# Diagonal blocks masked a strip at a time in a 2-D prefix-sum kernel, and a rearranged end

## The chip, the cores and the metric

The kernel runs on one core of one Trainium2 chip. The metric is the device time of one execution in microseconds, the median of several. A profile's span is about 1.7 us shorter than the time of the same run. Of the engines, TensorE does the matrix products, into an accumulator memory called PSUM; VectorE and ScalarE multiply, add and sum along rows; GpSimd issues the loads. The input is fp32 in memory; the kernel's strips hold it as bf16, a format of two bytes.

## The reference, cut to what matters

```python
B, H, W = 4, 4224, 4224                       # x is fp32
ps = np.cumsum(np.cumsum(x, axis=1), axis=2)
diag = np.diagonal(ps, axis1=1, axis2=2)
return np.cumsum(diag, axis=1)
```

Each of the four images must be read once: 4 x 4224 x 4224 x 4 bytes = 285.5 MB. The output is 68 KB. The diagonal at i needs the sum of every element whose row and column are both at most i; an element (r, c) first counts at max(r, c). The output is the running sum of that diagonal.

## The kernel before

A strip is 768 rows: 128 partitions, six rows each. It is loaded as bf16 (the load casts) by GpSimd's queue into one of three buffers. For a strip that starts at row r0, columns right of its diagonal block go through TensorE into column sums; columns left of it are summed along rows by ScalarE and VectorE; and the block on the diagonal is split by a mask `um` into the part above the diagonal (into the column sums) and the rest (into the row sums).

```python
NBUF = 3
strips = ctx.enter_context(tc.tile_pool(name="strips", bufs=NBUF))
mup = ctx.enter_context(tc.tile_pool(name="mup", bufs=3))
...
def masked(o, i, m, acc):                      # product and its row sums in one instruction
    nc.vector.scalar_tensor_tensor(out=o, in0=i, scalar=1.0, in1=m,
                                   op0=ALU.mult, op1=ALU.mult, accum_out=acc)
...
def add_up(strip, f, r0, acc, ums, wp=0, ws=None):
    nw = f * P // GW
    g = r0 // GW
    hi = r0 + f * P
    for j in range(g + nw, NG):                # right of the block: TensorE
        for q in range(f):
            columns(j, 0, GW, strip[:, q, j * GW : (j + 1) * GW])
    ...
    for q in range(f):                         # the block, one of the f rows at a time
        mu = mup.tile([P, F2 * P], BF16, name="mu")[:, : f * P]
        masked(mu, strip[:, q, r0:hi], ums[q], acc[:, q, 2:3])
        for h in range(nw):
            columns(g + h, 0, GW, mu[:, h * GW : (h + 1) * GW])
        if ws > wp:
            act_sum(acc[:, q, 0:1], strip[:, q, wp:ws])          # ScalarE
    row_sums(acc[:, :, 1], strip[:, :, ws:hi])                   # VectorE, masked part included
```

Later the masked sums are taken off again (`acc[..., 1] - acc[..., 2]`). TensorE works in program order: the masked matmuls of a strip stand behind all its unmasked ones (in the first strip of the old profile the 54 unmasked start at 36.06 us, the first masked one at 47.71). The six products of a strip share three `mu` buffers, so the fourth waits for TensorE to have read the first.

The last 128 rows of the last image come at the very end, in four blocks of 32 rows (0 to 3). They add to the last 128 outputs, and the 256 rows ahead of them to the last 384, through small one-row matmuls (`weigh`) in three PSUM tiles `fin_a`, `fin_m` and `fin_e`.

## Time and profile before

| what | value |
|---|---|
| time, median of 3 | 668.58 us |
| span of the profile | 666.7 us |
| load queue's busy share | 99.8% |
| VectorE busy | 335.7 us (50%) |
| TensorE busy | 215.4 us (32%) |
| ScalarE busy | 140.2 us (21%) |
| a full load, from issue to landing | 69.2 us, median |

How to read it: the engines are idle half of the time or more, and the transfers never are. The GB/s in the slices that follow count the bytes that land, as bf16 (142.47 MB for the load queue); the bytes read, in fp32, are twice that (285.47 MB), so that 217 GB/s there are 434 GB/s of reads. A load that takes 69 us to land, while one lands every 30 us, has spent more than half of that standing behind other loads. The wait that the change aims at is in the wait view of the old kernel (who waited for whom: total us, times, longest us):

```profile
DVE mu L257 <- DMA strip<-in_x_dram: 217.6, 20, 21.3
DVE mu L257 <- PE d L214: 91.2, 16, 9.5
```

The first line is VectorE waiting for data. The second is VectorE stopped in the middle of a strip's products until TensorE has freed a `mu` buffer.

### The profile page before, as it was taken

The numbers are of one execution on the slowest core, as the hardware profiler recorded it, in microseconds if no ns is written. First come the engines' busy times: TensorE is split into PE (matmuls) and PEld (weight loads), VectorE is DVE, ScalarE is ACT, GpSimd is POOL, SyncE is SP. The second block draws the span as 40 slices with busy tenths as digits, with TensorE's granted clock in tenths as the row PEclk, the third lists the DMA queues.
The fourth block names the chain that finished last, engine by engine and source line by source line (L and its number), as shares of the span: only waits on it lengthen the run. The fifth ranks groups of instructions, "written<-read, shape, count | busy, mean of one in ns | idle before, by whom it ended". The sixth has DMA issues, their size and how long they took to land.

```text
span 666.7 us, 2921 instructions
## 1 busy us (share of the span) xinstructions
PE 215.4 (32%) x1009; PEld 99.4 (15%) x1009; DVE 335.7 (50%) x381; ACT 140.2 (21%) x226; POOL 28.0 (4%) x61
## 2 busy tenths in 40 slices
PE   0071623403118153140321724404032254350426
PEld 0030211101003021010110312201011021120103
DVE  3023627276924351745782425265498241635776
ACT  0000121406300103040630020304063002030436
POOL 5000000000000000000000000000000000001000
PEclk9995858566558585765655958667565595765759
DMA  9999999999999999999999999999999999999998
GB/s 201 219 219 219 214 219 218 211 217 213 218 220 219 216 217 219 216 217 219 214 216 216 216 219 217 220 211 219 217 217 219 213 220 215 217 217 217 215 210 154
DMA packets 7673, 143.27 MB, mean 215 GB/s; under 512 B 702, under 2 KB 1002, under 8 KB 2154
## 3 DMA queue, kind: packets, MB, share of 16 engines
q0 software_dynamic: 7296, 142.47, 99.8%
q1 hardware_dynamic: 362, 0.61, 0.3%
q8 instruction: 8, 0.13, 0.1%
q14 instruction: 7, 0.06, 0.0%
HBM read 285.47 MB, written 0.07 MB: 428 GB/s over the span
## 4 chain that ended last, share of the span: by engine, by line
another core or an unknown queue 39%; DVE 24%; PE 21%; DMA 12%; issue 4%; POOL 0%; DVEq 0%; POOLq 0%
PE d L214 21%; DVE acc L240 16%; DMA strip<-in_x_dram 12%; DVE mu L257 6%; POOL strip L420 0%; DVE pu L240 0%; DVE c L257 0%; POOL strip L409 0%; DVE acc L343 0%; DVE acc L340 0%; PE carry_ps L214 0%; DVE rows L368 0%; DVEq L257 0%; PE fin_e L214 0%
## 5 line engine op out<-in xcount | busy, mean ns | idle before, releaser
L257 DVE SCALAR_TENSOR_TENSOR mu<-strip,um 128x768 bf16<-128x768 bf16 (+1 forms) x129 | 110.7, 908 | 308.9 <-DMA strip<-in_x_dram 217.6
L214 PE MATMUL d<-strip,sel 128*11 128x384 bf16 x603 | 138.9, 404 | 333.8 <-DMA strip<-in_x_dram 333.8
L235 ACT ACTIVATE dump<-strip 128x416 bf16<-128x416 bf16 (+8 forms) x112 | 128.3, 1146 | 523.0 <-DMA strip<-in_x_dram 520.3
L240 DVE TENSOR_REDUCE acc<-strip 128x6 f32<-128x4608 bf16 (+6 forms) x23 | 195.9, 8519 | 0.0
L214 PEld LDWEIGHTS <-sel 128*11 128x11 bf16 x849 | 86.2, 102 | 512.9 <-issue 475.3
L214 PE MATMUL d<-mu,sel 128*11 128x384 bf16 x243 | 59.6, 354 | 65.7 <-DVE mu L257 65.5
L76 POOL DMA_DIRECT2D strip<-in_x_dram x24 | 16.4, 686 | 555.9 <-DVE acc L240 415.4
L235 ACT ACTIVATION_READ_ACCUMULATOR dump<-strip 128x1 f32 x112 | 20.9, 186 | 0.0
L214 PE MATMUL d<-ident,rows 128*11 128x128 f32 x24 | 5.2, 379 | 17.2 <-DVE rows L377 16.4
L257 DVE DVE_READ_ACCUMULATOR mu<-strip,um 128x1 f32 x129 | 10.6, 82 | 0.0
L214 PE MATMUL fold<-strip,ident_h 128*128 128x480 bf16 x8 | 3.3, 589 | 8.6 <-DMA strip<-in_x_dram 8.6
L214 PEld LDWEIGHTS d<-ident,rows 128*11 128x11 f32 x24 | 2.5, 119 | 19.1 <-DVE rows L377 17.3
L214 PE MATMUL d<-halves,rows 128*11 128x64 f32 x48 | 5.3, 290 | 0.0
L214 PEld LDWEIGHTS d<-halves,rows 128*11 128x11 f32 x48 | 4.7, 127 | 1.8 <-issue 1.7
L240 DVE TENSOR_REDUCE pu<-d 11x1 f32<-11x384 f32 x4 | 2.2, 545 | 5.0 <-PE d L214 5.0
L214 PE MATMUL fold<-weights,quarter 32*128 32x128 f32 x2 | 0.8, 498 | 11.0 <-POOL quarter L200 11.0
L447 DVE TENSOR_TENSOR_SCAN c<-ones_row,carry,c 11x384 f32<-11x384 f32 x4 | 4.0, 1006 | 0.1
L447 DVE TENSOR_TENSOR_SCAN c<-ones_row,carry,d 11x384 f32<-11x384 f32 x4 | 4.0, 1001 | 0.1
L214 PEld LDWEIGHTS <-ident_h 128*128 128x128 bf16 x20 | 2.2, 114 | 12.0 <-issue 11.9
L420 POOL DMA_DIRECT2D strip<-in_x_dram x5 | 2.7, 552 | 21.5 <-DMA strip<-in_x_dram 21.5
L240 DVE TENSOR_REDUCE parts<-strip 128x3 f32<-128x3072 bf16 x1 | 3.4, 3350 | 0.0
L221 DVE COPY weights<-fold 128x128 f32<-128x128 f32 x1 | 0.3, 291 | 5.4 <-PE fold L214 5.4
(102 smaller groups left out, 44.4 us busy)
## 6 DMA issues: line engine op xcount, KB each, us to landing
strip<-in_x_dram POOLq DMA_DIRECT2D x19, 6336.0 KB, 69.2
strip<-in_x_dram POOLq DMA_DIRECT2D x5, 3168.0 KB, 55.2
strip<-in_x_dram POOLq DMA_DIRECT2D x1, 1080.0 KB, 45.0
strip<-in_x_dram POOLq DMA_DIRECT2D x1, 768.0 KB, 48.0
strip<-in_x_dram POOLq DMA_DIRECT2D x3, 256.0 KB, 49.2
head<-in_x_dram SPq DMA_DIRECT2D x1, 528.0 KB, 3.9
strip<-in_x_dram POOLq DMA_DIRECT2D x1, 192.0 KB, 43.7
strip<-in_x_dram POOLq DMA_DIRECT2D x1, 64.0 KB, 28.6
```

The source lines that it names most:

```text
L76: nc.gpsimd.dma_start(out=o, in_=x[b, r0 : r0 + f * P, :].rearrange("(p f) w -> p f w", f=f))
L214: nc.tensor.matmul(o, lhsT=lhsT, rhs=rhs, start=start, stop=False, skip_group_check=True)
L221: nc.vector.tensor_copy(out=weights4, in_=w4_ps)
L235: nc.scalar.activation(out=dump[:, :w], in_=src, func=ACT.Copy, accum_out=acc)
L240: nc.vector.reduce_sum(out=acc, in_=src, axis=AX.X)
L257: nc.vector.scalar_tensor_tensor(out=o, in0=i, scalar=1.0, in1=m, op0=ALU.mult, op1=ALU.mult, accum_out=acc,)
L420: nc.gpsimd.dma_start(out=part_b[:, sb, c0:c1], in_=x[b, r0 : r0 + R, :TB].rearrange("r (k c) -> r k c", k=4)[:, :, c0:c1],)
L447: nc.vector.tensor_tensor_scan(out=c12[:, i, :], data0=ones_row, data1=src, initial=carry[:, i : i + 1], op0=ALU.mult, op1=ALU.add,)
```

## The change

The intent: fewer and longer VectorE instructions with no wait on TensorE in mid-strip; one PSUM row of 384 columns (`fin`) and one of 32 (`fin_e`) in place of three pieces at the end; block 1 of the last rows summed by ScalarE and VectorE instead of TensorE. The core of the diff:

```diff
-    mup = ctx.enter_context(tc.tile_pool(name="mup", bufs=3))
+    mup = ctx.enter_context(tc.tile_pool(name="mup", bufs=1))
...
-            for q in range(f):
-                mu = mup.tile([P, F2 * P], BF16, name="mu")[:, : f * P]
-                masked(mu, strip[:, q, r0:hi], ums[q], acc[:, q, 2:3])
+            mu = mup.tile([P, f, f * P], BF16, name=f"mu{f}")
+            block = strip[:, :, r0:hi]
+            nc.vector.tensor_mul(out=mu, in0=block, in1=um)
+            nc.vector.tensor_sub(out=block, in0=block, in1=mu)
+            for q in range(f):
                 for h in range(nw):
-                    columns(g + h, 0, GW, mu[:, h * GW : (h + 1) * GW])
+                    columns(g + h, 0, GW, mu[:, q, h * GW : (h + 1) * GW])
...
-            nc.vector.tensor_sub(
-                out=acc[..., 1], in0=acc[..., 1], in1=acc[..., 2]
-            )
...                                             (the end)
-        fin_a = psum_s.tile([1, M0], FP32, name="fin_a")
-        fin_m = psum_s.tile([1, E0 - M0], FP32, name="fin_m")
+        fin = psum_s.tile([1, GW], FP32, name="fin")
...
-        for sb, cp in ((0, CB), (1, c1a)):
-            for c in range(0, cp, P):
-                matmul(by_ps[:, sb * R :], part_b[:, sb, c : c + P], ...)
+        for c in range(0, CB, P):
+            matmul(by_ps, part_b[:, 0, c : c + P], weights4_h, start=c == 0)
...
+        for k, ca in ((0, 512), (1, 448)):      # blocks 1 and 2
+            act_sum(bsum[:, k, 0:1], part_b[:, k + 1, :ca])
+            pair_sum(bsum[:, k, 1:2], part_b[:, k + 1, ca:])
+            if k == 1:
+                finish(0, M0)
+            row_sums(btot[:, k : k + 1], bsum[:, k])
+            weigh(btot[:, k : k + 1], weights4, M0 + (k + 1) * R)
```

The difference is written back into the strip, so the plain row reduction that follows needs no correction. The mask tile now holds all six rows' masks (4608 columns instead of 773). Left out of the cut: each pair sum writes into a tile of its own instead of a shared one, and the sums of the 256 rows in `fold_a` take 256 columns of a row in one matmul instead of 128.

More of the change, by code (lines that the diff above doesn't have):

```diff
@@ L91, in upper_mask @@
     def upper_mask(f):
-        w = f * P
-        wide = consts.tile([P, w + f - 1], BF16, name=f"um{f}")
-        nc.vector.memset(wide, 1.0)
+        um = consts.tile([P, f, f * P], BF16, name=f"um{f}")
+        nc.vector.memset(um, 1.0)
         nc.gpsimd.affine_select(
-            out=wide,
-            in_=wide,
+            out=um,
+            in_=um,
             compare_op=ALU.is_gt,
             fill=0.0,
-            base=1 - f,
-            pattern=[[1, w + f - 1]],
+            base=0,
+            pattern=[[-1, f], [1, f * P]],
             channel_multiplier=-f,
         )
-        return [wide[:, f - 1 - q : f - 1 - q + w] for q in range(f)]
+        return um
     um6 = upper_mask(F2)
@@ L240, in row_sums @@
         nc.vector.reduce_sum(out=acc, in_=src, axis=AX.X)
+    pairs = []
     def pair_sum(acc, src):
         w = src.shape[-1] // 2
-        pair = dumpool.tile([P, 512], FP32, name="pair")
+        pair = last.tile([P, 288], FP32, name=f"pair{len(pairs)}")
+        pairs.append(pair)
         nc.vector.scalar_tensor_tensor(
@@ L312, in columns, with add_up @@
             first[0] = False
-        def add_up(strip, f, r0, acc, ums, wp=0, ws=None):
+        def add_up(strip, f, r0, acc, um, wp=0, ws=None):
             nw = f * P // GW
@@ L332, in add_up @@
             row_sums(acc[:, :, 1], strip[:, :, ws:hi])
-        acc6 = smalls.tile([P, NS, F2, 3], FP32, name="acc6")
-        acc3 = smalls.tile([P, 2, F, 3], FP32, name="acc3")
+        acc6 = smalls.tile([P, NS, F2, 2], FP32, name="acc6")
+        acc3 = smalls.tile([P, 2, F, 2], FP32, name="acc3")
         nc.vector.memset(acc6[:, 0, :, 0], 0.0)
@@ L388 @@
             fold_in(fold_g, strip[:, F:], 0, wp, 160, start=True)
-            parts = last.tile([P, F, 4], FP32, name="parts")
+            parts = last.tile([P, F, 3], FP32, name="parts")
             add_up(strip[:, F:], F, T0 - GW, parts, um3, wp, ws)
-            nc.vector.tensor_scalar_mul(
-                out=parts[:, :, 2], in0=parts[:, :, 2], scalar1=-1.0
-            )
-            row_sums(parts[:, :, 3], fold_g)
+            row_sums(parts[:, :, 2], fold_g)
             row_sums(r3[:, row_of(LG - 1), :], parts)
@@ L425 @@
                 )
-            fold_a = psum_s.tile([P, 2, P], FP32, name="fold_a")
+            fold_a = psum_s.tile([P, 2, 256], FP32, name="fold_a")
             c0, c1 = acuts[0]
             cp, ca = c0 + 768, c0 + 768 + 1152
-            fold_in(fold_a, part_a, c0, cp, P, start=True)
+            fold_in(fold_a, part_a, c0, cp, 256, start=True)
             for h in range(2):
@@ L465 @@
         cp = c0 + 768
-        fold_in(fold_a, part_a, c0, cp, P)
+        fold_in(fold_a, part_a, c0, cp, 256)
         for h in range(2):
@@ L475 @@
         E0 = GW - R
-        fin_a = psum_s.tile([1, M0], FP32, name="fin_a")
-        fin_m = psum_s.tile([1, E0 - M0], FP32, name="fin_m")
+        fin = psum_s.tile([1, GW], FP32, name="fin")
         fin_e = psum_s.tile([1, R], FP32, name="fin_e")
         yl = last.tile([1, GW], FP32, name="yl")
-        def weigh(rows, w, r0, fins, start=False):
-            for fin, f0, f1 in fins:
-                g0 = max(f0, r0)
-                if g0 < f1:
-                    matmul(
-                        fin[:, g0 - f0 :], rows, w[:, g0 - r0 : f1 - r0], start=start
-                    )
@@ L490, in finish, with weigh @@
-        def finish(fin, c0, c1):
+        def weigh(rows, w, r0, start=False):
+            matmul(fin[:, r0:], rows, w[:, : GW - r0], start=start)
+        def finish(c0, c1):
             nc.vector.tensor_add(
-                out=yl[:, c0:c1], in0=fin, in1=c12[0:1, 1, c0:c1]
+                out=yl[:, c0:c1], in0=fin[:, c0:c1], in1=c12[0:1, 1, c0:c1]
             )
         by_ps = psum_s.tile([P, P], FP32, name="fold")
-        c1a = CB // 2
-        for sb, cp in ((0, CB), (1, c1a)):
-            for c in range(0, cp, P):
-                matmul(
-                    by_ps[:, sb * R :],
-                    part_b[:, sb, c : c + P],
-                    weights4_h[:, : P - sb * R],
-                    start=sb == 0 and c == 0,
-                )
@@ L507 @@
-        bsum = last.tile([P, 3], FP32, name="bsum")
-        act_sum(bsum[:, 0:1], part_b[:, 1, c1a:])
+        for c in range(0, CB, P):
+            matmul(by_ps, part_b[:, 0, c : c + P], weights4_h, start=c == 0)
         by = last.tile([P, P], FP32, name="by")
         nc.scalar.copy(out=by, in_=by_ps)
-        fins = ((fin_a, 0, M0), (fin_m, M0, E0), (fin_e, E0, GW))
-        weigh(arows[:, 0:1], weights, 0, fins[:1], start=True)
-        weigh(arows[:, 1:2], weights, P, fins[:1])
-        weigh(arows[:, 0:1], weights, 0, fins[1:], start=True)
@@ L516 @@
-        weigh(arows[:, 1:2], weights, P, fins[1:])
-        weigh(dtot, weights, M0, fins)
-        weigh(bsum[:, 0:1], weights4, M0 + R, fins)
-        weigh(ones_col, by, M0, fins)
-        finish(fin_a, 0, M0)
-        act_sum(bsum[:, 1:2], part_b[:, 2, :448])
-        pair_sum(bsum[:, 2:3], part_b[:, 2, 448:])
-        for k in (1, 2):
-            weigh(bsum[:, k : k + 1], weights4, M0 + 2 * R, fins)
+        weigh(arows[:, 0:1], weights, 0, start=True)
+        weigh(arows[:, 1:2], weights, P)
@@ new lines @@
+        weigh(ones_col, by, M0)
+        weigh(dtot, weights, M0)
+        bsum = last.tile([P, 2, 2], FP32, name="bsum")
+        btot = last.tile([P, 2], FP32, name="btot")
+        for k, ca in ((0, 512), (1, 448)):
[5 more added lines that the diff above has]
+            weigh(btot[:, k : k + 1], weights4, M0 + (k + 1) * R)
@@ L533 @@
         for k in (1, 0, 2):
-            weigh(esum[:, k : k + 1], weights4, E0, fins)
-        finish(fin_m, M0, E0)
+            matmul(fin_e, esum[:, k : k + 1], weights4[:, :R], start=k == 1)
+        finish(M0, GW)
         nc.sync.dma_start(
@@ L538 @@
         )
-        finish(fin_e, E0, GW)
-        nc.sync.dma_start(out=out[b, T0 + E0 : N].unsqueeze(0), in_=yl[:, E0:])
+        ye = last.tile([1, R], FP32, name="ye")
+        nc.vector.tensor_add(out=ye, in0=fin_e, in1=yl[:, E0:])
+        nc.sync.dma_start(out=out[b, T0 + E0 : N].unsqueeze(0), in_=ye)
 _INS = ['x']
```

## The prediction

> **What bounds the kernel now.** I read the page's slices first, because they tell whether one resource is full all the time. The columns are 40 equal slices of the 666.7 us span; the digits are tenths of busy time, then GB/s.
>
> ```profile
> DVE  3023627276924351745782425265498241635776
> ...
> DMA  9999999999999999999999999999999999999998
> GB/s 201 219 219 219 214 219 218 211 217 213 218 220 219 216 217 219 216 217 219 214 216 216 216 219 217 220 211 219 217 217 219 213 220 215 217 217 217 215 210 154
> ...
> q0 software_dynamic: 7296, 142.47, 99.8%
> ```
>
> The transfers are full in every slice, VectorE is half idle. A strip of 768 rows by 4224 fp32 columns is 12.98 MB of reads. In the chain of work (start, duration, what) the first strips land where the piece before TensorE's matmuls ends:
>
> ```profile
> 1.33 34.69 DMA strip<-in_x_dram
> 36.06 12.15 PE d L214 x56
> ...
> 65.95 8.93 PE d L214 x44
> ...
> 95.94 7.34 PE d L214 x32
> ...
> 125.81 5.81 PE d L214 x20
> ```
>
> The landings are 29.9 us apart, which is 12.98 MB / 29.9 us = 434 GB/s. They do not come closer while the engines idle: between 15 and 35 us nothing computes, and the transfers run as they do later.
>
> The next question is whether a transfer ever waits for a buffer. The wait view blames VectorE for long idle times of GpSimd, which issues the loads, but an issue is late only if the queue has run dry. The timeline of GpSimd gives the issues:
>
> ```profile
> 56.36 0.77 POOL L76 DMA_DIRECT2D strip<-in_x_dram  x1 [45.42 <-DVE acc L240]
> ...
> 146.26 0.70 POOL L76 DMA_DIRECT2D strip<-in_x_dram  x1 [29.96 <-DVE acc L240]
> 175.06 0.71 POOL L76 DMA_DIRECT2D strip<-in_x_dram  x1 [28.10 <-DVE acc L343]
> ```
>
> At 56.36 the strips landing at 65.95 and 95.94 are already queued: 39.6 us of spare time. The tightest are 146.26, where the half strip behind the landing at 155.68 should end near 170.6 (half of 29.9 later), 24 us to spare, and 175.06, where the next strip lands at 200.57, 25 us. So no buffer ever limits the transfers. The end, from the same chain:
>
> ```profile
> 619.74 43.68 DMA strip<-in_x_dram
> ...
> 663.51 0.29 DVE pair L246
> ...
> 663.97 0.57 PE fin_e L214 x6
> ...
> 664.56 0.18 DVE yl L491
> ```
>
> The last data count as landed at 663.4, and the span ends 3.3 us later. Only three things can move the time: the transfers' start, their rate, and these 3.3 us.
>
> **What the Trainium skill says.** "VectorE: DVE Perf Modes", section "The perf-mode tier table", gives a bf16 tensor_tensor in SBUF two elements a cycle (1224 ns for 2048) and tensor_reduce one. The page's fp32 tensor_tensor formula, (N+151)/0.96 ns, fits this trace's one-element-a-cycle operations: 957 for 768 elements against 955 ns measured for the masking product, 4957 for 4608 against 4950 for the reduction. This trace has no large bf16 tensor_tensor, so its double rate is unconfirmed here. "DMA: Bandwidth & Descriptors", section "Where 436 GB/s comes from", puts the ceiling of the core's transfer ports at 435 GB/s; the trace has 434, so the stream is at it. "SBUF — State Buffer", section "SBUF: two separate sides", says that engine and DMA accesses use disjoint ports, and warns that GpSimd cannot write descriptors while VectorE holds a shared port in a two-port mode; a two-input VectorE operation holds it only against a GpSimd operation that reads SBUF. The even landings agree with the first. The old product has two SBUF inputs too, so the change adds no new kind of holding.
>
> **The change, part by part.** *Masks.* Removed are 114 products of 768 columns and 15 of 384 with their 129 accumulator reads: 103.1 + 7.6 + 10.6 = 121.3 us. Added are, for 19 strips and 5 three-row pieces, one product and one difference each. At two elements a cycle I estimate from the skill's figure (2304+151)/0.96 = 2.56 us and, for 1152 elements, 0.76 us: 38 x 2.56 + 10 x 0.76 = 104.9 us. The larger mask tiles cost (5760 - 1159)/0.96 ns = 4.8 us more of memset at the start. VectorE goes from 335.7 to about 319 us. What matters more, its wait in mid-strip goes: the old product cycles through three buffers and waits for TensorE (91.2 us in 16 waits in the wait view), the new one has a tile for the whole strip. In the first strip the reduction would end at 36.04 + 2 x 2.56 + 4.95 = 46.1 instead of 55.8. The buffer then waits for TensorE instead: its masked matmuls begin at 47.7, and twelve at 0.19 us (1.14 us for six) end at 50.0. The next load is issued some 6 us earlier, behind 46 us of queued transfers instead of 39.6. It lands when it did before. Gain: 0.
>
> *Setup.* The masks' select on GpSimd covers 5760 elements instead of 1159, which took 1.31 us: about 6.5, so 5.2 more, plus some 3 us of waiting for the longer memset. GpSimd's constants end near 19 instead of 11 us, long before the first landing at 36, and behind the three first loads. Cost: 0.
>
> *The end.* The landings of the last blocks stay near 661.2, 662.5, 663.45 and, for the last quarter-width piece, some 0.3 later. Block 1 now costs ScalarE 0.63 + 0.19 us and VectorE about 0.4 us beside each other, ready at 662.1 by the rows of the timeline, and a small reduction of 0.17 us. TensorE loses four matmuls of block 1 and the split of each weighing in up to three: the one-row sums are 384, 256, 128 and 128 columns. The old 256 + 128 columns began at 661.52 and were over at 662.06; in that proportion 896 columns need 1.26 us. They can begin at 661.0, when the row totals exist, because block 1's matmuls no longer stand ahead: done by 662.3. Then on VectorE: block 2's pair sum 662.6 to 663.05; the first 256 outputs, which now stand behind it (0.41 us, before it in the old order), to 663.45; a small reduction to 663.6, where ScalarE's sum is ready at 663.24; then the two pair sums of block 3, 0.1 later than before; the addition of 128 outputs beside TensorE's last matmul; and the last addition of 32. Sum for the tail: +0.1 us, within -0.1 and +0.6.
>
> Together 668.6 + 0 + 0.1 = **668.7 us**.
>
> **Rivals.** (1) *VectorE's saving comes out in the time.* For it: releases come earlier, and the chain gives VectorE 24%. It would mean up to 16 us, 652 us. Against it: 24 us to spare at the tightest issue, and the transfers already at 434 GB/s. I give it hardly a chance. (2) *The double rate does not come.* Each product or difference costs 4.96 us, VectorE rises to about 407 us (61%). Per strip that is 9.9 instead of 5.9 us, 4 us later at most, inside the 24 us. Only the last three-row piece, at 649.9, could push on: 1.3 us there, which reach the row totals at 661.9 instead of 660.9. The time would be 669 to 669.7. (3) *GpSimd is shut out while VectorE runs the long two-input operations.* A few us on an issue with 24 to spare: 0. (4) *VectorE's new order at the end exceeds the landings' spacing of 1.2 us.* The four last operations are back to back; each further wait on TensorE or ScalarE adds 0.2 to 0.4: 669.2.
>
> **Range and chances.** The runs before spread from 668.11 to 668.94. To this I add the tail, -0.1 to +1, and as much again as the runs' spread for the transfers of another session: 667.4 to 670.0. A change of over 2% is 13 us. Faster would need fewer bytes or a higher rate, slower a dry queue; the changed kernel moves the same bytes in the same order. 1% faster, 98% within, 1% slower.
>
> **What would show it right or wrong.** Right: 29.9 us between landings, 99.8% for the load queue, the first landing at 36.0; two VectorE rows of about 2.56 and 0.76 us; no wait of the product on TensorE in mid-strip; loads issued about 6 us earlier after the first strip with a longer median from issue to landing; last data near 663.4, end of span 3.2 to 3.9 us later. Wrong: landings further apart than 30.1 us, a slice of the transfers below 9 before the last, rows of 4.9 us, or a tail above 4 us, where the wait just ahead of the last additions names the term.

## The result

The changed kernel takes 668.48 us (median of 6 runs, 667.20 to 671.07), the old one beside it 668.55 (6 runs, 668.10 to 669.11). The ratio is 1.000, 95% interval 0.998 to 1.002. A ratio here and below is the mean time of one kernel's fast runs over that of the other's of the same rounds, so it is not quite the ratio of the medians quoted. Executions over 1.5% slower than the fastest of the same kernel are left out of the means. The change is worth nothing that these runs can see.

The slices of the changed kernel's page, span 665.7 us, answer to those of the old one in the prediction:

```profile
DVE  3161625456916153454782524436288333352867
...
DMA  9999999999999999999999999999999999999998
GB/s 203 219 219 219 219 218 218 219 209 212 219 221 218 218 218 219 218 218 216 209 218 220 218 216 218 219 218 218 218 213 215 219 217 215 219 217 218 218 205 161
...
q0 software_dynamic: 7296, 142.47, 99.9%
```

The transfers are as full as before and their bytes are the same. On VectorE, the instruction groups (count, then busy us and the mean ns of one, then idle time before them and what ended it):

```profile
L329 DVE TENSOR_TENSOR mu<-strip,um 128x4608 bf16<-128x4608 bf16 x19 | 48.6, 2558 | 300.7 <-DMA strip<-in_x_dram 300.7
L330 DVE TENSOR_TENSOR strip<-strip,mu 128x4608 bf16<-128x4608 bf16 x19 | 48.6, 2558 | 0.9
```

The predicted 2.56 us is 2558 ns. All the idle time ahead of the product is for data; the 91.2 us for TensorE are gone. The timeline of GpSimd (start, duration, the idle time ahead and what ended it) shows what this does to the loads:

```profile
46.66 0.78 POOL L76 DMA_DIRECT2D strip<-in_x_dram  x1 [29.49 <-PE d L213]
...
142.36 0.70 POOL L76 DMA_DIRECT2D strip<-in_x_dram  x1 [31.48 <-DVE acc L239]
174.33 0.72 POOL L76 DMA_DIRECT2D strip<-in_x_dram  x1 [31.27 <-ACT dump L234]
```

What gave the first of these buffers back shows in TensorE's timeline (first the unmasked matmuls, which read the strip, then the masked ones, which read the `mu` tile):

```profile
34.86 11.50 PE L213 MATMUL d<-strip,sel 128*11 128x384 bf16 x54 [16.85 <-DMA strip<-in_x_dram]
46.20 2.11 PE L213 MATMUL d<-mu,sel 128*11 128x384 bf16 x12
```

The first strip landed at 34.8 us, and its buffer was given back 11.8 us later; in the old kernel it was 56.36 - 36.06 = 20.3 us. The earlier issue bought nothing. The page's list of loads (count, KB, median us from issue to landing), first of the old kernel, then of the changed one:

```profile
strip<-in_x_dram POOLq DMA_DIRECT2D x19, 6336.0 KB, 69.2
```

```profile
strip<-in_x_dram POOLq DMA_DIRECT2D x19, 6336.0 KB, 76.5
```

By the median, the loads are issued some 7 us earlier and stand 7 us longer in the queue. They land every 29.9 us either way (single gaps are longer, in both: at most 30.15 us between two neighbouring full strips of the old profile, 30.54 of the changed one). That is where the gain went.

### The profile page after: what moved, and what is told of

The parts are those of the page before. It is cut to its first block, busy times and chain, and to the rows that moved or that the text cites. A ratio compares the mean times of both kernels' runs of the same rounds, so it can differ in the third digit from the quotient of the medians.

```text
span 665.7 us, 2561 instructions
## 1 busy us (share of the span) xinstructions
PE 204.8 (31%) x979; PEld 98.2 (15%) x979; DVE 334.6 (50%) x166; ACT 140.3 (21%) x226; POOL 32.0 (5%) x61
## 4 chain that ended last, share of the span: by engine, by line
DVE 47%; another core or an unknown queue 44%; DMA 5%; PE 2%; issue 1%; DVEq 0%; POOLq 0%
DVE acc L239 29%; DVE mu L329 8%; DVE strip L330 8%; DMA strip<-in_x_dram 5%; PE d L213 1%; DVE c L445 1%; PE fold L213 1%; DVE pu L239 0%; PE fin L213 0%; DVE c L259 0%; DVE rows L369 0%; DVE acc L344 0%; PE carry_ps L213 0%; DVE carry L443 0%
## 5 line engine op out<-in xcount | busy, mean ns | idle before, releaser
L329 DVE TENSOR_TENSOR mu<-strip,um 128x4608 bf16<-128x4608 bf16 (+1 forms) x24 | 52.4, 2183 | 305.8 <-DMA strip<-in_x_dram 305.7
L213 PE MATMUL d<-mu,sel 128*11 128x384 bf16 x243 | 49.1, 355 | 45.8 <-DVE mu L329 45.8
L330 DVE TENSOR_TENSOR strip<-strip,mu 128x4608 bf16<-128x4608 bf16 (+1 forms) x24 | 52.4, 2183 | 1.0
L213 PE MATMUL fold<-strip,ident_h 128*128 128x480 bf16 x8 | 3.4, 598 | 10.6 <-DMA strip<-in_x_dram 10.6
L213 PE MATMUL fold<-weights,quarter 32*128 32x128 f32 x2 | 0.8, 496 | 17.2 <-POOL quarter L199 17.2
L94 DVE MEMSET um<- 128x4608 bf16 (+1 forms) x2 | 4.9, 2458 | 1.1 <-issue 1.1
L95 POOL TENSOR_SCALAR_AFFINE_SELECT um<-um 128x4608 bf16<-128x4608 bf16 (+1 forms) x2 | 5.2, 2608 | 2.4 <-DVE um L94 2.4
## 6 DMA issues: line engine op xcount, KB each, us to landing
strip<-in_x_dram POOLq DMA_DIRECT2D x19, 6336.0 KB, 76.5
```

What stands on the lines that cost most here:

```text
L94: nc.vector.memset(um, 1.0)
L95: nc.gpsimd.affine_select(out=um, in_=um, compare_op=ALU.is_gt, fill=0.0, base=0, pattern=[[-1, f], [1, f * P]], channel_multiplier=-f,)
L213: nc.tensor.matmul(o, lhsT=lhsT, rhs=rhs, start=start, stop=False, skip_group_check=True)
L329: nc.vector.tensor_mul(out=mu, in0=block, in1=um)
L330: nc.vector.tensor_sub(out=block, in0=block, in1=mu)
```

## The experiments

Eleven experiments ran, the last of them the changed kernel once more, all correct, on three chips. "Old" is the kernel before, "changed" the kernel after.

### Each half of the change alone, and the wait alone

*e1_masks_only*: the new masks with the old end.

```diff
 (old, with)
+            nc.vector.tensor_mul(out=mu, in0=block, in1=um)
+            nc.vector.tensor_sub(out=block, in0=block, in1=mu)
 (and the rest of the masks; everything from fold_a on, and pair_sum, as in the old kernel)
```

> The new masks with the old end. Theory (the stream of transfers sets the time and has 24 us to spare at its tightest): 668.5 us within the runs' spread, landings 29.9 us apart, VectorE busy about 334 us, loads of full strips landing some 76 us after their issue as in the changed kernel (69 in the old). Rival (the masks gain and the new end gives it back): 665 or less here, and more than 670 with the new end alone.

*e2_tail_only*: the old masks with the new end.

```diff
 (old, with everything from fold_a on, and pair_sum, as in the changed kernel)
+        fin = psum_s.tile([1, GW], FP32, name="fin")
```

> The old masks with the new end. Theory: 668.5 us within the runs' spread, last landing to end of span 3.2 to 3.4 us as in both kernels, loads landing 69 us after issue. Rival (the new end costs what the masks gain): over 670. If the first landing at 34.8 us (36.0 in the old kernel) belongs to the longer setup of the new masks, it is near 36.0 here and near 34.8 with the new masks; if it is chance, it is in no order.

*e3_six_mu*: one line of the old kernel.

```diff
-    mup = ctx.enter_context(tc.tile_pool(name="mup", bufs=3))
+    mup = ctx.enter_context(tc.tile_pool(name="mup", bufs=6))
```

> The old kernel with six mask buffers instead of three, nothing else. Theory: VectorE's wait on TensorE in mid-strip (91.2 us in 16 waits) goes almost wholly, loads land about 76 us after their issue instead of 69, and the time stays 668.5. Rival (those 91 us are on the path): tens of us faster.

Measured, beside the old kernel's 668.87 us (11 runs, 668.15 to 671.08): masks alone 669.60 (ratio 1.0003, 0.9986 to 1.0020), end alone 668.20 (0.9989, 0.9976 to 1.0003), six buffers 669.65 (1.0007, 0.9989 to 1.0024). All three are the same as the old kernel. So no gain of one half is eaten by a loss of the other.

In e1 and in e3 VectorE's wait for TensorE in mid-strip is gone from the wait view, and in both a full load takes longer from issue to landing: 76.5 and 76.4 us, against 70.0 in e2, which keeps the old masks. The only wait of the product that is left in e3, and its list of loads:

```profile
DVE mu L257 <- DMA strip<-in_x_dram: 311.7, 20, 22.1
...
strip<-in_x_dram POOLq DMA_DIRECT2D x19, 6336.0 KB, 76.4
```

One line moves the loads as much as the whole new masking does, and neither moves the time. VectorE's busy time in e1 is 333.8 us, as expected.

### More bytes

*e4_more_bytes*: the changed kernel, one more load of 128 rows per whole image into rows that nothing reads.

```diff
             load_rows(strip[:, :F], b, T0)
+            load_rows(strip[:, F : F + 1], b, 0)
```

> The changed kernel with 2.163 MB more read per whole image, into rows of a strip buffer that nothing reads (three loads, 6.49 MB, no further work for an engine). Theory: 6.49 MB at 434 GB/s are 14.95 us, so 683.4 us. Rival (an engine or a wait for a buffer sets the time, the stream has slack): clearly less than 15 us more, down to 0.

Measured: 683.01 us (682.25 to 684.05), 14.1 us above the old kernel's 668.87 of the same call (ratio 1.0204, so 13.6 us by the means; interval 12.4 to 14.9). Nearly all of the 14.95 us that the bytes take at 434 GB/s appears in the time. The transfers are the bound; in a kernel bound by an engine the added bytes, on which no engine works, should have cost little.

### More work for VectorE

*e5_after_two*: the changed kernel, two useless reductions per full strip.

```diff
+            if f == F2:
+                waste = dumpool.tile([P, F2], FP32, name="waste")
+                for _ in range(2):
+                    row_sums(waste, strip[:, :, r0:hi])
             row_sums(acc[:, :, 1], strip[:, :, ws:hi])
```

> The changed kernel with two reductions of 4608 elements more per full strip, 4.95 us each: 19 x 9.9 = 188 us more of VectorE, 80% busy. Theory: 668.5 us still, since VectorE's work per image, about 85 + 50 = 135 us, stays below the 164.6 us that an image's transfers take. Rival (VectorE's work is on the path at least in part): anything from 10 to 188 us more.

Measured: 673.80 us (672.50 to 675.16) beside 669.23, ratio 1.0065 (1.0041 to 1.0089). Of 188 us more work, about 4.5 us come out in the time. The expectation, that none would, was wrong, and the timeline of VectorE in the changed kernel, without the extra work, says why:

```profile
643.67 0.17 DVE L386 COPY rows<-acc 128x3 f32<-128x3 f32 x1
648.85 0.76 DVE L329 TENSOR_TENSOR mu<-strip,um 128x1152 bf16<-128x1152 bf16 x1 [5.01 <-DMA strip<-in_x_dram]
```

Here VectorE has finished the last full strip and the first three-row piece and waits 5.01 us for the last piece. That is all its spare time at the end. The last full strip's 9.9 us more push 4.9 us past it. In e5's own profile TensorE shows the landing of that piece, and VectorE comes to it 4.75 us later:

```profile
650.70 3.36 PE L213 MATMUL fold<-strip,ident_h 128*128 128x480 bf16 x8 [0.85 <-DMA strip<-in_x_dram]
```

```profile
655.45 0.76 DVE L329 TENSOR_TENSOR mu<-strip,um 128x1152 bf16<-128x1152 bf16 x1
```

What comes after then runs late to the end of the span. The landings stay 29.9 us apart (650.70 is 1.9 us later than in the changed kernel's profile only because the first landing was, 36.79 for 34.86). An average over an image, which is what I had computed, hides this: a strip in mid-stream has the next strips to make up for it, the last one has not.

*e6_after_five* and *e7_before_five*: the same with five reductions, in the changed kernel and in the old one, so that VectorE is the bound.

```diff
-                for _ in range(2):
+                for _ in range(5):
```

> The changed kernel with five such reductions per full strip, 24.8 us: VectorE's work per image is about 208 us, above the 164.6 us of its transfers, so that VectorE must become the bound. Theory: about 830 us, VectorE over 95% busy, transfers no longer full. It is run to be compared with the old kernel under the same load.

> The old kernel with the same five reductions per full strip. With VectorE as the bound, the difference from the changed kernel is what the change saves of VectorE. Theory from the start-to-start times of the records (six products 0.885 us apart, 5.31 us, against a product and a difference of 2.60 each, 5.19): 19 x 0.12, the rest small, 2 to 4 us longer than the changed kernel under the same load. As in the prediction (accumulator reads counted as time of their own): 16 us longer. If the mid-strip wait on TensorE persists under this load: up to 91 us longer; I expect it gone, since TensorE has its unmasked columns done before VectorE comes to the strip.

Measured: 846.62 us for the changed kernel (846.06 to 847.37) and 882.57 for the old one (881.71 to 883.83). Under this load the change is worth 36 us. The expectation for the old kernel was an excess of 2 to 4. (The 830 us expected for the changed one took VectorE as busy throughout; it idled for 43 us of the span, from 801.5 to 844.8.) From the two pages, e6 first, then e7: line 1 (busy us and share of the span) and VectorE's slices.

```profile
PE 220.0 (26%) x979; PEld 102.3 (12%) x979; DVE 801.5 (95%) x261; ACT 140.2 (17%) x226; POOL 32.0 (4%) x61
...
DVE  4399999999989999999998999999999899999997
```

```profile
PE 239.6 (27%) x1009; PEld 101.0 (11%) x1009; DVE 801.7 (91%) x476; ACT 140.2 (16%) x226; POOL 28.0 (3%) x61
...
DVE  2189999999969999999995999999999699979997
```

VectorE does the same amount of work in both, 801.5 and 801.7 us. The change saves it waiting. The wait view of e7 has the rest:

```profile
DVE mu L257 <- PE d L214: 33.3, 5, 8.8
```

I had expected this wait to be gone under load, because TensorE would be through its unmasked columns before VectorE came to the strip. That holds for strips within an image. At the start of an image it does not: TensorE's first matmuls of the new image stand behind the last small ones of the old, which wait for VectorE, so both start on the first strip together and VectorE then waits through TensorE's 54 unmasked matmuls. (In the first image both start together on the first landing; the fifth wait, 4.6 us at the third strip of the last image, again follows a small matmul that had waited for VectorE.)

*e9_before_five_six_mu* tells whether that wait is the whole difference.

```diff
 (e7, with)
-    mup = ctx.enter_context(tc.tile_pool(name="mup", bufs=3))
+    mup = ctx.enter_context(tc.tile_pool(name="mup", bufs=6))
```

> The old kernel with five more reductions per full strip and six mask buffers. Under that load the old kernel took 882.6 us and the changed one 846.6; VectorE's busy time was the same (801.7 and 801.5), and the wait view of the old one has 33.3 us of waits for TensorE between mask products. Theory (these waits are the difference): they go, and the time is 882.6 - 33.3 = about 849 us. Rival (the products themselves, or the difference taken in place of accumulators, save the 36 us): it stays near 882.

Measured: 847.81 us (847.33 to 849.80), on another chip than e6 and e7; the old kernel took 668.21 there and 669.23 beside them. In its wait view the product waits for data alone:

```profile
DVE mu L257 <- DMA strip<-in_x_dram: 22.3, 1, 22.3
```

So 34.8 of the 36 us go with the wait, and six small buffers are enough to remove it; the long product and the in-place difference are not needed for it. The 1.2 us that are left are about what the two chips differ by in the old kernel, so what the product itself saves, if anything, is not shown.

### Two strip buffers

*e8_two_buffers*: the changed kernel.

```diff
-    NBUF = 3
+    NBUF = 2
```

> The changed kernel with two strip buffers instead of three. Theory of the queue's slack: full strips are released 12 to 17 us after they land, less than the 29.9 us of the next transfer, but the fifth strip's release 19.2 us after landing finds a half strip of only 14.95 us ahead of it, so the queue runs dry for 4.3 us and the 0.5 to 1.5 us of an issue, once per whole image: 3 x 5 = 15 us, 684 us. If buffers were already short with three: far more.

Measured: 692.61 us (691.92 to 693.65), ratio to the old kernel 1.0347, 23 us more by the means. The queue does run dry once per whole image, where expected, but for longer. The timeline of GpSimd gives the issue, TensorE's the landing (the start of the matmuls that waited for the load), and between them stands, from ScalarE's, the landing of the half strip ahead:

```profile
175.83 0.70 POOL L76 DMA_DIRECT2D strip<-in_x_dram  x1 [31.28 <-ACT dump L234]
```

```profile
171.54 1.99 ACT L234 ACTIVATE dump<-strip 128x2144 bf16<-128x2144 bf16 x1 [4.38 <-DMA strip<-in_x_dram]
```

```profile
209.83 5.49 PE L213 MATMUL d<-strip,sel 128*11 128x384 bf16 x24 [22.32 <-DMA strip<-in_x_dram]
```

From issue to landing are 34.0 us for a transfer that takes 29.9 in a full queue: 4.1 us more on an empty one, where I had put 0.5 to 1.5 (34.0 and 33.6 us in the next two images). The half strip ahead landed at 171.54, so the queue is behind by 209.83 - 171.54 - 29.9 = 8.4 us; three times that is 25 us, for the 23 measured. With three buffers this never happens, in either kernel.

### The end, and the spread between runs

In e2 the end took longer than expected: from the landing of the last quarter row to the end of the span 4.2 us, not 3.2 to 3.4. The stretches of the last 2.5 us ahead of that landing (columns: length; busy us and count of TensorE, its weight loads, VectorE, ScalarE and GpSimd; granted TensorE clock, as a share of full speed; transfers' share; GB/s), of the changed kernel and of e2:

```profile
659.96:662.46 2.50, 1.84 (x10) 0.76 (x10) 1.42 (x8) 1.39 (x5) 0.00 (x0) 1.00 0.84 145
```

```profile
660.97:663.47 2.50, 2.38 (x6) 0.67 (x7) 1.12 (x6) 1.43 (x5) 0.00 (x0) 0.50 0.52 86
```

The granted clock is 1.00 in one and 0.50 in the other. The Trainium skill, "TensorE: Matmul & The Clock Gate", section "What's actually happening", has these two states, set by a window of recent activity that runs free of the kernel; the traces agree that there are two and that the same code meets either. TensorE's matmuls with the row totals take 1.24 us in the one and 2.29 in the other (timelines of TensorE, the changed kernel and then e2), and VectorE waits for them (third, e2's timeline of VectorE):

```profile
660.32 1.24 PE L213 MATMUL fin<-weights,arows 128*1 128x384 f32 x4 [0.79 <-DVE arows L239]
```

```profile
661.09 2.29 PE L214 MATMUL fin<-weights,arows 128*1 128x384 f32 x4 [0.39 <-DVE arows L240]
```

```profile
664.26 0.41 DVE L488 TENSOR_TENSOR yl<-fin,c 1x256 f32<-1x256 f32 x1 [1.31 <-PE fin L214]
...
664.66 0.37 DVE L249 SCALAR_TENSOR_TENSOR pair<-strip 128x224 f32<-128x224 bf16 x1
```

The pair sum of the last block, whose data were there at 663.47, starts at 664.66 because the addition ahead of it waits for TensorE. *e10_one_addition* moves that addition behind the pair sums.

```diff
-            if k == 1:
-                finish(0, M0)
...
-        finish(M0, GW)
+        finish(0, GW)
```

> The changed kernel with the first 256 outputs' addition moved behind the last pair sums and joined with the other 128, so that VectorE does not wait for TensorE ahead of the last data. In the profiles where TensorE's granted clock was 0.5 in the last microseconds, the end took 4.2 and 4.6 us from the last quarter row's landing instead of 3.2. Theory (that wait holds the pair sums up): 3.4 us where the clock is 1.0 (the longer addition, 0.15), under 4.0 where it is 0.5; the time within 0.1% of the changed kernel. Rival (TensorE itself is late at the low clock, whatever VectorE does): 4.2 or more at the low clock.

*e11_after_again* is the changed kernel once more.

> The changed kernel unchanged, for a second profile and five more rounds on another chip beside the old kernel. Theory: within 0.2% of the old kernel, 667 to 671 us; first landing between 34.8 and 36.9 us with no relation to the kernel; tail 3.2 us at a granted clock of 1.0 in the last microseconds, over 4 at 0.5.

Measured beside the old kernel's 668.21 us (9 runs, 668.01 to 669.48): e10 668.44 (ratio 1.0001, 0.9989 to 1.0014), e11 668.24 (1.0000, 0.9988 to 1.0013). The e10 profile met the low clock, 0.52, and the same 2.29 us of matmuls; its end took 3.53 us, which fits the wait as the cause of the longer ends. It is one profile, and the medians don't show a gain. The clock is not all that moves the end either: e1's took 3.56 us at the full clock (table below). No version tried beats either kernel.

The profiles of the kernels that move the same bytes with three strip buffers and no added work, cut at two points (the first strip's landing; the landing of the last quarter row, where ScalarE's last sum starts):

| run | first landing | to the last quarter row | to the end | clock in the last 2.5 us ahead of it | span |
|---|---|---|---|---|---|
| old | 36.06 | 627.44 | 3.20 | 1.00 | 666.7 |
| changed | 34.86 | 627.60 | 3.24 | 1.00 | 665.7 |
| e1, new masks, old end | 35.05 | 627.39 | 3.56 | 1.00 | 666.0 |
| e2, old masks, new end | 35.51 | 627.96 | 4.23 | 0.50 | 667.7 |
| e3, old, six buffers | 36.82 | 628.07 | 4.01 | 0.50 | 668.9 |
| e10, one addition | 34.58 | 627.89 | 3.53 | 0.52 | 666.0 |
| e11, changed again | 36.74 | 628.30 | 3.06 | 1.00 | 668.1 |

The middle column, 94% of the time, is the same for all within 0.15%. The spread between profiles comes for the most part from the first landing (34.6 to 36.8 us) and from the end (3.1 to 4.2), beside 0.9 us in the middle, and none of them goes with a kernel: the changed kernel has both 34.86 and 36.74, and the old end meets the low clock too (e3). So the 1.0 us by which the changed kernel's profile is shorter than the old one's is not the change. Why the first load takes longer in some executions these runs don't tell.

## Why the prediction was right

The time was to be 668.7 us within 667.4 to 670.0, and it is 668.5. That holds for the median; three of the six single runs (667.20, 667.37 and 671.07) lie outside, so that a hit within 0.2 us is in part luck. What was not luck is the reason given, that no wait on the path was touched. By its own steps:

- **The transfers bound it.** Right, and now shown by dose: more bytes lengthen the time by almost their own transfer time (e4), 188 us of VectorE work by about 4.5 (e5), and the removal of 91 us of waits by nothing (e3). The prediction also sets its 434 GB/s against a ceiling of the transfer ports. The 434 are bytes read; half of them, 217, land in the kernel's strips. That the rate stays at 434 whether the engines idle or work is shown; that the stream stands at that ceiling is not. The sign of being wrong, landings more than 30.1 us apart, was set too tight: the old profile has one gap of 30.15, the changed one 30.54.
- **24 us to spare at the tightest issue.** Nothing contradicts it, and e8 shows a tight place behind the fifth strip, one of the two that were named. The 0.5 to 1.5 us that I then put for the restart of a dry queue were 4.1.
- **VectorE from 335.7 to about 319 us.** Wrong: 334.6. The step that failed is "103.1 + 7.6 + 10.6 = 121.3 us" removed. It adds records that overlap. In the old kernel's timeline the products of 768 columns last 0.955 us but start 0.88 apart, and the read of the accumulator lies inside the next product:

```profile
36.93 0.08 DVE L257 DVE_READ_ACCUMULATOR mu<-strip,um 128x1 f32 x1
36.93 0.95 DVE L257 SCALAR_TENSOR_TENSOR mu<-strip,um 128x768 bf16<-128x768 bf16 x1
37.81 0.08 DVE L257 DVE_READ_ACCUMULATOR mu<-strip,um 128x1 f32 x1
37.81 0.95 DVE L257 SCALAR_TENSOR_TENSOR mu<-strip,um 128x768 bf16<-128x768 bf16 x1
```

The removed time is about 114 x 0.88 + 15 x 0.48 = 107.5 us, the added 104.8, and the longer memsets take 4.9 instead of 1.1. Nothing is left of it; the 1.1 us less on the page are of the size of the subtractions of the masked sums (1.5 us), which went too. e6 and e7 confirm it with 801.5 and 801.7 us. The sum for 319 also leaves out the prediction's own 4.8 us of memset: by its terms it is 324.
- **The double rate.** Right: 2558 ns for the 2557 estimated, 757 to 759 for 757. Rival (2) falls. (Its 407 us don't follow from its terms: 335.7 - 121.3 + 38 x 4.96 + 10 x 1.36 are 416.)
- **The mid-strip wait goes, and the load is issued 6 us earlier.** The direction was right, the size 8.5 us (11.8 after the landing instead of 20.3). The step that failed is "The buffer then waits for TensorE instead: its masked matmuls": these read the `mu` tile, not the strip. The strip is free after the unmasked matmuls, and the issue at 46.66 follows them.
- **Setup costs nothing.** Right: the constants were ready at 17.2 us (19 predicted), and the first landing did not move with them.
- **The end, +0.1 us within -0.1 and +0.6.** Right at the same clock: 3.24 for 3.20. The sum had no term for the granted clock, which adds about a microsecond to either end when it is low (4.0 in e3, 4.2 in e2). The range of the time had room for it, with a tail of up to +1 us. TensorE's 1.26 us for 896 columns were too short: the 662.06 that they rest on is where the last of the old records starts (662.1 in the view of tile `fin_a`), not where it ends; measured were 1.51 (660.32 to 661.83, the start of the next matmul), and VectorE's first addition waited 0.26 us for TensorE.
- **Rivals (1), (3) and (4).** A gain of up to 16 us did not come, and GpSimd's issues last as long as before (688 ns for 686). Rival (4), one more wait on TensorE at the end, is what e2's profile shows at the low clock; the changed kernel's two profiles, both at 1.00, end in 3.24 and 3.06 us.

## What to carry to other kernels

When every load is issued well before the ones queued ahead of it have landed (here 24 us at the least), an earlier release of its buffer only lengthens its stay in the queue: compare the time from issue to landing before and after, not the idle time of the issuing engine. To know what a change to an idle engine is worth, load that engine until it is the bound; here the change's 36 us then came almost wholly from one wait that three more small buffers remove too. Don't add up an instruction's record and its accumulator read as if they followed each other: take start-to-start times, and ask separately how much slack the engine has ahead of the last data.

## What the Trainium skill lacked or had wrong

- "DMA: Bandwidth & Descriptors", section "Anatomy of one DMA", gives about 2.0 us of fixed cost for a DMA from GpSimd's queue. On a queue that had run dry, a load of 12.98 MB took 34.0 us from issue to landing instead of 29.9 in a full queue, 4.1 us more (e8; 3.7 to 4.1 in its three images).
- No page says which bytes count when a load casts. Here fp32 read and bf16 written ran at 434 GB/s by the bytes read and 217 by the bytes written.
- "VectorE: DVE Perf Modes", section "The DRAIN you can't avoid", has the next operation wait for the pipe to empty, with a reference to when it starts earlier, and no figure for an accumulator read. Here products of 768 columns with records of 0.955 us start 0.88 us apart, and the accumulator read, a record of 0.08 us of its own, costs nothing in the sequence. The page's rates themselves held: 2558 ns measured for the 2557 estimated from its tensor_tensor figure.
